# Gate/up, down and the last gate with output chunks in fours: products of 400 columns, and one part of the operand held while 512 weight columns pass

## The chip, the cores and the metric

The kernel runs on one core of one Trainium2 chip. The number that counts is the device time of one execution in microseconds (us), here as the median of several runs. Of the engines the text says PE for the matrix engine, ACT for the scalar engine, DVE for the vector engine; PEld is the loading of weights into the PE array, which the profile shows as a row of its own for each product. A "product" is one matmul instruction; its "columns" are those of its moving operand. "Native" products have fp32 operands; the others have operands in fp32r, a rounded 32-bit form of which the kernel writes a high part and a low part.

## What is computed

One decoder layer over 264 tokens: 256 of a prompt and 8 single-token sequences. Attention and a state-space group read one projection of the normed input; their results go through an output projection into the residual; then come a gated feed-forward block and a last gate. The stages that the change touches are the three last matrix stages:

```
h  = rms_norm(x, g_pre_ffn)
gu = h @ w_gate_up                                    # 2048 -> 2 x 5632
f  = (silu(gu[..., :D_FF]) * gu[..., D_FF:]) @ w_down # 5632 -> 2048
x  = x + rms_norm(f, g_post_ffn)
x  = x + sigmoid(x @ w_ple_gate) * (pe @ w_ple_proj)  # 2048 -> 2048
```

## The kernel before

Everything is kept transposed: a tile has 128 features on the partitions and the 264 tokens (`T`) as its columns. A matrix stage makes its output in chunks of 128 features, one PSUM bank for each (tile `acc`), and goes over the contraction in blocks of 128 (`k`). The stages of `stream_plan` are, in order: in, oa and os (the output projection), pp (first half), gu (gate/up: 88 chunks of 16 blocks), dn (down: 16 chunks of 44 blocks), pp (second half), pg (last gate: 16 chunks of 16 blocks). The 128x128 weight blocks are laid out in the order in which they are used, eight to a unit of 512 KB; there are 362 units of which the first six are used in native fp32.

Weights and operands are split, so that the products keep more than fp32r's precision: ACT writes the high part of a unit (`wh<-raw`, in `w_high`), DVE the rest (`wl<-raw,wh`, in `w_low`). The operand of a stage has a high tile and a low tile as well: `hh` and `hl` for gu, the two halves of `f0`/`f1` for dn, `x2h` and `x2l` for pg. For each weight block `stream` issues three products of 264 columns, all with the weight block as the stationary operand:

```
mm(ps, hi[:, b], xh, 0.1205, start=first, stop=False)
mm(ps, hi[:, b], xl, 0.1205, start=False, stop=False)
mm(ps, lo[:, b], xh, 0.1205, start=False, stop=last)
```

Most chunks are made one after the other (`chunks`); the first six of gu and of pg go side by side (`together`, with `EARLY`), block by block, while their operand is still being made. When a chunk is finished its epilogue runs: `epi_gu` multiplies a gate chunk and an up chunk out of PSUM by the norm factor (DVE tiles `gs` and `uu`, which frees both banks), applies SiLU on ACT, multiplies, and writes the two parts of `f`; `epi_dn` squares the chunk on ACT, copies it to `o2` and adds the square to `ssq_o` on DVE; `epi_pg` ends in the output.

The order of all instructions on all engines is set when the kernel is built: `Pace` keeps a clock for each engine and gives each piece of work that could go next a start time by costs that stand in the code (0.1205 for a product of 264 columns); the earliest goes first. PSUM banks are counted in `acc` and `bk`, 8 together. On the chip each engine keeps that order and waits on semaphores.

Between dn and pg stand the 16 pp products of the second half (eight chunks of two blocks, 48 products). In that stretch the chain that makes pg's operand must run: the last chunk's square, its sum over the partitions on PE (`ps_o<-sqd`), `rstd` on ACT and DVE (`n_y`, `n_t`, `Ro`), then for each block two DVE operations on `o2`, the high part `x2h` on ACT and the low part `x2l` on DVE.

## Time and profile before

| what | us |
|---|---|
| median of 3 runs | 1198.21 (1197.01 to 1201.53) |
| the profiled execution, its own time | 1203.08 |
| its span, first to last instruction | 1201.3 |
| PE busy / PEld busy | 1181.2 / 1154.4 |
| DVE busy / ACT busy | 754.0 / 587.1 |

The span is what the profile shows of one execution; the time of that execution is a little longer than its span. Products are pipelined on PE, so that rows overlap: a product's duration includes the way through the array, and what a product costs in a dense stretch is the distance from its start to the next one's start. Busy times of DVE and ACT can be read as they stand.

### The profile page before, as it was taken

To read this page: it belongs to the slowest core of one execution; us is meant where nothing else is said; L and a number is where in the kernel's file an instruction comes from. 1 tells how busy PE (TensorE), PEld (TensorE's weight loads), DVE (VectorE), ACT (ScalarE), POOL (GpSimd) and SP (SyncE) were. 2 spreads that over 40 slices of the span, in tenths; PEclk is the share of its full clock that TensorE was granted. 3 is DMA by queue.
4 is the path that set the end of the run, shared out by engine and by line. 5 is a ranking of instruction groups with operands and counts; after the bars stand their busy time and mean duration, and the time that the engine had idled before them with its cause. 6 is when DMAs were issued, how large, how long until landed. Compare 5 with 4: busy or idle time off the path is not lost.

```text
span 1201.3 us, 23874 instructions
## 1 busy us (share of the span) xinstructions
PE 1181.2 (98%) x9699; PEld 1154.4 (96%) x9699; DVE 754.0 (63%) x1325; ACT 587.1 (49%) x911; POOL 53.2 (4%) x97
## 2 busy tenths in 40 slices
PE   9899999999999999999999999999999999999998
PEld 7788888999999999999999999999999999999998
DVE  8998888867897555555555555555444444446864
ACT  6476857645665444444444444444434444435542
POOL 1122232000000000000000000000000000000000
PEclk9899999999999999999999999999999999999999
DMA  8745646666676666655555555555766666666683
GB/s 266 248 147 166 186 155 183 187 194 222 195 264 179 186 180 179 188 179 182 184 180 182 187 177 180 188 178 187 252 179 181 185 178 180 188 176 204 211 251 112
DMA packets 102214, 228.96 MB, mean 191 GB/s; under 512 B 26999, under 2 KB 50519, under 8 KB 101591
## 3 DMA queue, kind: packets, MB, share of 16 engines
q1 hardware_dynamic: 102103, 227.43, 61.6%
q8 instruction: 76, 1.25, 0.4%
q14 instruction: 35, 0.29, 0.1%
HBM read 214.60 MB, written 12.80 MB: 189 GB/s over the span
## 4 chain that ended last, share of the span: by engine, by line
PE 88%; DVE 7%; DMA 2%; ACT 1%; issue 1%; POOL 0%; SPq 0%; DVEq 0%; POOLq 0%; ACTq 0%
PE acc L285 82%; PE py L285 2%; DVE wl L222 1%; PE px L289 1%; DVE X L222 1%; DMA gt<-ys 1%; DVE rt L222 1%; DMA xtab<-in_xtab 0%; DMA xr<-in_x 0%; DVE ssq_x L222 0%; PE ph L975 0%; DVE sc L222 0%; DVE xl L222 0%; ACT s L281 0%; PE o L285 0%
## 5 line engine op out<-in xcount | busy, mean ns | idle before, releaser
L222 DVE TENSOR_TENSOR wl<-raw,wh 128x1024 fp32r<-128x1024 f32 x362 | 442.4, 1223 | 302.8 <-PE acc L285 281.3
L281 ACT ACTIVATE wh<-raw 128x1024 fp32r<-128x1024 f32 x362 | 383.8, 1060 | 449.2 <-PE acc L285 434.4
L285 PE MATMUL acc<-hh,wh 128*128 128x264 f32 x1408 | 399.5, 284 | 0.0
L285 PE MATMUL acc<-hl,wh 128*128 128x264 f32 x1408 | 398.3, 283 | 0.5 <-DVE hl L236 0.5
L285 PE MATMUL acc<-hh,wl 128*128 128x264 f32 x1408 | 398.5, 283 | 0.0
L285 PEld LDWEIGHTS acc<-hl,wh 128*128 128x128 f32 x1408 | 265.0, 188 | 0.8 <-DVE hl L236 0.7
L285 PEld LDWEIGHTS acc<-hh,wh 128*128 128x128 f32 x1408 | 265.2, 188 | 0.0
L285 PEld LDWEIGHTS acc<-hh,wl 128*128 128x128 f32 x1408 | 264.0, 188 | 0.0
L285 PE MATMUL acc<-f,wh 128*128 128x264 f32 x1408 | 256.8, 284 | 0.0
L285 PEld LDWEIGHTS acc<-f,wh 128*128 128x128 f32 x1408 | 217.8, 188 | 0.1
L285 PE MATMUL acc<-f,wl 128*128 128x264 f32 x704 | 199.7, 284 | 0.0
L285 PEld LDWEIGHTS acc<-f,wl 128*128 128x128 f32 x704 | 132.5, 188 | 0.0
L285 PE MATMUL acc<-x2h,wh 128*128 128x264 f32 x256 | 72.9, 285 | 0.0
L285 PE MATMUL acc<-x2h,wl 128*128 128x264 f32 x256 | 72.5, 284 | 0.0
L285 PE MATMUL acc<-xh,wh 128*128 128x264 f32 x240 | 72.5, 302 | 0.0
L285 PE MATMUL acc<-x2l,wh 128*128 128x264 f32 x256 | 71.9, 284 | 0.0
L285 PE MATMUL acc<-xl,wh 128*128 128x264 f32 x240 | 68.9, 287 | 2.3 <-DVE xl L222 2.3
L285 PE MATMUL acc<-xh,wl 128*128 128x264 f32 x240 | 68.7, 286 | 0.0
L222 DVE TENSOR_TENSOR uu<-acc,Rf 128x264 f32<-128x264 f32 x44 | 19.0, 432 | 50.6 <-PE acc L285 50.6
L285 PEld LDWEIGHTS acc<-xl,wh 128*128 128x128 f32 x240 | 46.0, 192 | 3.3 <-DVE xl L222 2.7
L285 PE MATMUL acc<-aops,wh 128*128 128x264 f32 x256 | 49.0, 291 | 0.0
L285 PEld LDWEIGHTS acc<-x2h,wh 128*128 128x128 f32 x256 | 48.1, 188 | 0.2 <-ACT ppt L281 0.2
(324 smaller groups left out, 1349.1 us busy)
## 6 DMA issues: line engine op xcount, KB each, us to landing
raw<-in_w SPq DMA_DIRECT2D x367, 512.0 KB, 3.6
T<-td SPq DMA_DIRECT2D x8, 512.0 KB, 4.6
xs<-in_x SPq DMA_DIRECT2D x2, 1056.0 KB, 7.1
ppd<-ppt SPq DMA_DIRECT2D x16, 132.0 KB, 3.2
x1d<-oo SPq DMA_DIRECT2D x4, 528.0 KB, 5.0
x<-x1d SPq DMA_DIRECT2D x2, 1056.0 KB, 7.3
ppr<-ppd SPq DMA_DIRECT2D x16, 132.0 KB, 4.0
xtab<-in_xtab SPq DMA_DIRECT2D x8, 256.0 KB, 3.0
```

Source lines behind the costliest of these rows:

```text
L222: V.tensor_tensor(out=out, in0=in0, in1=in1, op=op)
L281: S.activation(out=out, in_=in_, func=func, **kw)
L285: PE.matmul(out, lhsT, rhs, start=start, stop=stop)
L289: PE.transpose(out, in_, ident)
```

## The change

In gu, dn and pg the chunks go in groups of four, one weight block of each at a time. The operand of these stages now lies as one tile with the high part in columns 0 to 263 and the low part in columns 264 to 527 (`ha`/`hb`, `f0`/`f1`, `x2a`/`x2b`; `wide`). For four weight blocks of one contraction block there are now nine products in place of twelve:

- four of 400 columns ("a"): the high weights with the high part and the first 136 columns (`XE`) of the low part, written side by side into one bank;
- four of 264 columns ("b"): the low weights with the high part;
- one of 512 columns ("x"): the last 128 columns of the low part are the stationary operand, and the four high weight blocks pass as the moving operand. Its result stands the other way round (tokens on the partitions), in a bank of its own (`rows`).

At a group's end the rows bank is copied to SBUF by ACT (`held`), four products with a unit matrix ("c", 128 columns) add it, turned round, to the chunks' banks, and before the epilogue `whole` adds the 136 columns that stand apart: ACT copies them to `ext`, DVE adds them to the chunk. The last unit of a group is reordered (`last`) so that the rows are done early. Six chunks at the opening of gu and of pg go as one four and two in the old way (`six`); gu's chunks 3 and 47, and chunks 6 and 15 of pg, go in the old way; the last group of dn is a group of three beside one chunk in the old way. There are 28 groups.

In dn the last four chunks are copied to `o2` only after their squares. The write of `x1d` is a task of its own (`keep`).

The diff, cut to its core:

```diff
 def stream_plan():
...
+    def quad(at, gid, n=4):
+        r = []
+        for s in at:
+            r += [("a", s + i) for i in range(n)] + [("b", s + i) for i in range(n)] + [("x", s, gid)]
+            r += [("p", s + i) for i in range(n, 4)]
+        return r
+
+    def last(at, gid, between=(), n=4):
+        r = [("x", s, gid) for s in at] + list(between)
+        for i in range(n):
+            for s in at:
+                r += [("a", s + i), ("b", s + i)]
+            if i >= 2:
+                r += [("c", gid, j) for j in ((0, 1, 2) if i == 2 else (3,))]
+        return r + [("p", s + i) for i in range(n, 4) for s in at]
...
-    together("gu", EARLY["gu"], 16)
-    chunks("gu", [m for f in range(3, KF) for m in (f, KF + f) if m not in EARLY["gu"]], 16)
-    chunks("dn", range(16), KF)
+    six("gu", [0, KF, 1, KF + 1, 2, KF + 2], 16)
+    chunks("gu", [3, KF + 3], 16)
+    for f in range(4, KF, 2):
+        four("gu", [f, KF + f, f + 1, KF + f + 1], 16)
+    for m in range(0, 16, 4):
+        four("dn", list(range(m, m + 4)), KF, 4 if m < 12 else 3)
     chunks("pp", range(8, 16), 2)
-    together("pg", EARLY["pg"], 16)
-    chunks("pg", [m for m in range(16) if m not in EARLY["pg"]], 16)
+    six("pg", [0, 1, 2, 3, 4, 5], 16)
+    chunks("pg", [6], 16)
+    for m in (7, 11):
+        four("pg", list(range(m, m + 4)), 16)
+    chunks("pg", [15], 16)
...
+    def whole(ps):
+        yield "act", "+ext"
+        e = mid([P, XE], F32, "ext", "ext", 2)
+        act(e, ps[:, T:])
+        yield "dve"
+        add(ps[:, 0:XE], ps[:, 0:XE], e)
+        pace.rel("ext")
+
+    def held(gid):
+        yield "act"
+        rows[gid] = mid([P, 512], F32R, "rows", "rows", 2)
+        n = P * len(GROUPS[gid][1])
+        act(rows[gid][:, 0:n], rbank.pop(gid)[:, 0:n])
+        pace.rel("acc")
+        pace.sig(f"rows{gid}", "act")
...
+                        if what == "a":
+                            mm(ps, hi[:, b], x[:, 0:T + XE], 0.169, start=first, stop=False)
...
+                        elif what == "b":
+                            mm(ps[:, 0:T], lo[:, b], x[:, 0:T], 0.1205, start=False, stop=False)
+                        elif what == "x":
+                            n = P * len(GROUPS[more[0]][1])
+                            mm(ps[:, 0:n], x[:, T + XE:], hi[:, P * slot:P * slot + n], 0.422e-3 * n, start=first, stop=last)
...
+                        mm(ps[:, XE:T], rows[gid][:, P * j:P * j + P], ops["identr"], 0.1205, start=False)
```

How the instructions stand on the engines, before and after. First place: PE in the middle of gu, before. The rows are products, out<-moving,stationary, with the columns at the end; numbers tell buffers apart, and `acc_7630` and `acc_7691` are two chunks.

```order
L285 MATMUL acc_7630<-hh_4237,wh_7569 128x264
L285 MATMUL acc_7630<-hl_3642,wh_7569 128x264
L285 MATMUL acc_7630<-hh_4237,wl_7608 128x264
L285 MATMUL acc_7691<-hh_4237,wh_7603 128x264
L285 MATMUL acc_7691<-hl_3642,wh_7603 128x264
L285 MATMUL acc_7691<-hh_4237,wl_7636 128x264
```

The same place after the change: one contraction block of a group of four chunks. In the last row the weights are the moving operand.

```order
L358 MATMUL acc_5386<-hb_4239,wh_5465 128x400
L358 MATMUL acc_5390<-hb_4239,wh_5465 128x400
L358 MATMUL acc_5398<-hb_4239,wh_5465 128x400
L358 MATMUL acc_5400<-hb_4239,wh_5465 128x400
L358 MATMUL acc_5386<-hb_4239,wl_5489 128x264
L358 MATMUL acc_5390<-hb_4239,wl_5489 128x264
L358 MATMUL acc_5398<-hb_4239,wl_5489 128x264
L358 MATMUL acc_5400<-hb_4239,wl_5489 128x264
L358 MATMUL rows_5409<-wh_5465,hb_4239 128x512
```

Three products to a weight block, all of 264 columns, have become nine to four weight blocks. In all PE issues 1517 products fewer: the three stages had 7104 of 264 columns and now have 2720 of 264, 2188 of 400, 516 of 512 and 44 of 384, 8 of 136 (the "a" products of the two openings are cut in two) and 111 closing products of 128.

Second place: the end of a gu group after the change, on PE (the closing products of one group and the next group's first products).

```order
L358 MATMUL acc_5155<-identr_3643,rows_5362 128x128
L358 MATMUL acc_5159<-identr_3643,rows_5362 128x128
L358 MATMUL acc_5167<-identr_3643,rows_5362 128x128
L358 MATMUL acc_5169<-hb_4239,wh_5280 128x400
L358 MATMUL acc_5169<-hb_4239,wl_5306 128x264
```

After these rows the last two repeat for the second block, the fourth closing product follows, and then the next group's four products of 400, four of 264 and its first into a new rows bank. On DVE, at the same group's end (`ext` is the ACT copy of the 136 columns, and `uu` frees the two banks that it and `gs` read):

```order
L295 TENSOR_TENSOR wl_5354<-raw_5269,wh_5328 128x1024
L295 TENSOR_TENSOR acc_5155<-acc_5155,ext_5375 128x136
L295 TENSOR_TENSOR acc_5159<-acc_5159,ext_5378 128x136
L295 TENSOR_TENSOR gs_5392<-acc_5155,Rf_4241 128x264
L295 TENSOR_TENSOR uu_5393<-acc_5159,Rf_4241 128x264
L295 TENSOR_TENSOR acc_5167<-acc_5167,ext_5388 128x136
L295 TENSOR_TENSOR wl_5407<-raw_5293,wh_5352 128x1024
```

Two adds now stand ahead of `gs` and `uu`, where `gs` and `uu` stood alone; and a whole group ends at once, where chunks ended one by one.

Third place: PE between dn and pg, before, from dn's last product on (`ppo` is the operand of pp; x2 is two products alike).

```order
L285 MATMUL acc_12722<-f1_4864,wl_12811 128x264
L285 MATMUL acc_12896<-ppo_3741,wh_12809 128x264 x2
L285 MATMUL acc_12896<-ppo_3741,wl_12841 128x264
L285 MATMUL acc_12896<-ppo_3741,wh_12809 128x264 x2
L285 MATMUL acc_12896<-ppo_3741,wl_12841 128x264
L285 MATMUL acc_12908<-ppo_3741,wh_12809 128x264 x2
L285 MATMUL acc_12908<-ppo_3741,wl_12841 128x264
L285 MATMUL ps_o_12751<-sqd_12900,onesd_84 128x264
```

And after the change, around the same sum:

```order
L358 MATMUL acc_11914<-ppo_3743,wl_11828 128x264
L358 MATMUL ps_o_11924<-ssq_o_10140,onesd_84 128x264
L358 MATMUL ps_o_11924<-sqd_11904,onesd_84 128x264
L358 MATMUL acc_11914<-ppo_3743,wh_11800 128x264 x2
L358 MATMUL acc_11914<-ppo_3743,wl_11828 128x264
```

Of the 48 pp products 9 stood ahead of `ps_o<-sqd` and 39 behind it; now 27 stand ahead and 21 behind it.

## Rows read from the trace of the kernel before

**Rows 1.** The page: busy time of PE, and the chain that ended last.

```profile
PE 1181.2 (98%) x9699; PEld 1154.4 (96%) x9699; DVE 754.0 (63%) x1325; ACT 587.1 (49%) x911; POOL 53.2 (4%) x97
...
PE 88%; DVE 7%; DMA 2%; ACT 1%; issue 1%; POOL 0%; SPq 0%; DVEq 0%; POOLq 0%; ACTq 0%
PE acc L285 82%; PE py L285 2%; DVE wl L222 1%; PE px L289 1%; DVE X L222 1%; DMA gt<-ys 1%; DVE rt L222 1%; DMA xtab<-in_xtab 0%; DMA xr<-in_x 0%; DVE ssq_x L222 0%; PE ph L975 0%; DVE sc L222 0%; DVE xl L222 0%; ACT s L281 0%; PE o L285 0%
```

**Rows 2.** Windows: length, busy of PE, PEld, DVE, ACT, POOL; PEclk, DMA, GB/s.

```profile
600.00:700.00 100.00, 100.00 (x830) 100.00 (x829) 54.18 (x68) 42.25 (x51) 0.00 (x0) 1.00 0.56 183
900.00:1000.00 100.00, 100.00 (x826) 100.00 (x825) 43.91 (x40) 41.17 (x48) 0.00 (x0) 1.00 0.63 180
```

**Rows 3.** The page's groups: products of gu, dn and pg.

```profile
L285 PE MATMUL acc<-hh,wh 128*128 128x264 f32 x1408 | 399.5, 284 | 0.0
...
L285 PE MATMUL acc<-f,wh 128*128 128x264 f32 x1408 | 256.8, 284 | 0.0
...
L285 PE MATMUL acc<-f,wl 128*128 128x264 f32 x704 | 199.7, 284 | 0.0
...
L285 PE MATMUL acc<-x2h,wh 128*128 128x264 f32 x256 | 72.9, 285 | 0.0
```

**Rows 4.** By tile: duration of products in ns, min/median/max.

```profile
L285 PE MATMUL acc<-hh,wl x1408: 278/283/294, 327.4 to 839.6; 128*128 128x264 f32 x176
L285 PE MATMUL acc<-f,wl x704: 278/283/290, 840.0 to 1096.6; 128*128 128x264 f32 x176
```

**Rows 5.** By tile: the same of native products, two records each.

```profile
L285 PE MATMUL acc<-xt,raw x96: 386/386/490, 6.7 to 30.8; 128*128 128x264 f32 x96
```

**Rows 6.** Timeline of PE, native products: start, length, how many records.

```profile
27.47 3.72 PE L285 MATMUL acc<-xt,raw 128*128 128x264 f32 x16
```

**Rows 7.** Timeline of PE around 45 us.

```profile
45.10 0.42 PE L285 MATMUL acc<-xl,wh 128*128 128x264 f32 x1
...
46.86 0.42 PE L285 MATMUL acc<-xh,wh 128*128 128x264 f32 x1
```

**Rows 8.** Windows: the same stretch.

```profile
44.80:46.90 2.10, 2.10 (x12) 2.10 (x11) 2.10 (x9) 1.06 (x1) 0.00 (x0) 0.50 0.44 104
```

**Rows 9.** Timeline of PEld around a wait at gu's opening.

```profile
331.55 0.19 PEld L285 LDWEIGHTS acc<-hh,wh 128*128 128x128 f32 x1
332.48 0.19 PEld L285 LDWEIGHTS acc<-hl,wh 128*128 128x128 f32 x1 [0.74 <-DVE hl L236]
```

**Rows 10.** By tile: the product at 331.67, the last ahead of that wait.

```profile
L285 PE MATMUL acc<-hh,wh x1: 279/279/279, 331.7 to 331.7; 128*128 128x264 f32 x1
```

**Rows 11.** Timeline of PEld: weight loads of 128 columns for products of 128 columns.

```profile
97.39 1.86 PEld L285 LDWEIGHTS py<-G,SB 128*128 128x128 f32 x16 [0.17 <-issue]
```

**Rows 12.** Groups on ACT.

```profile
L281 ACT ACTIVATE wh<-raw 128x1024 fp32r<-128x1024 f32 x362 | 383.8, 1060 | 449.2 <-PE acc L285 434.4 <-DMA raw<-in_w 11.6 <-issue 2.5
...
L281 ACT ACTIVATE gy<-py 128x512 f32<-128x512 f32 x8 | 4.8, 599 | 8.4 <-PE py L285 8.3
...
L281 ACT ACTIVATE ht<-ph 128x128 f32<-128x128 f32 x8 | 2.2, 275 | 1.0 <-PE ph L975 1.0
```

**Rows 13.** Groups on DVE.

```profile
L222 DVE TENSOR_TENSOR wl<-raw,wh 128x1024 fp32r<-128x1024 f32 x362 | 442.4, 1223 | 302.8 <-PE acc L285 281.3 <-issue 14.3 <-ACT wh L281 2.8
L222 DVE TENSOR_TENSOR uu<-acc,Rf 128x264 f32<-128x264 f32 x44 | 19.0, 432 | 50.6 <-PE acc L285 50.6
...
L222 DVE TENSOR_TENSOR t<-p,xtab 128x128 f32<-128x128 f32 x8 | 2.3, 288 | 4.9 <-PE p L289 4.9
```

**Rows 14.** Timeline of PE between dn and pg.

```profile
1096.58 0.29 PE L285 MATMUL acc<-f,wl 128*128 128x264 f32 x1
...
1097.80 0.61 PE L285 MATMUL ps_o<-sqd,onesd 128*128 128x264 f32 x2
...
1102.96 0.28 PE L285 MATMUL acc<-x2h,wh 128*128 128x264 f32 x1
```

**Rows 15.** Timeline of ACT in the same stretch: the first high parts of pg's operand.

```profile
1101.88 0.77 ACT L281 ACTIVATE x2h<-o 128x264 fp32r<-128x264 f32 x2
```

More of the change, by code (lines that the diff above doesn't have):

```diff
@@ L393, in build @@
     ops = {}
+    wide = {}
     XF = {}
@@ L1516, in need_op, with finish, end @@
             return f"x2_{k}"
+        def finish(nm, m, ps):
+            ready = pace.t["pe"] + 0.2
+            def end():
+                if (nm, m) in FOURS:
+                    yield from whole(ps)
+                yield from EPI[nm](ps[:, 0:T], m)
+            pace.add(end(), ready=ready, prio=PRIO["epi"])
         def stream():
@@ L1544, in stream @@
                     yield "pe", need
+                    if not native:
+                        lo = lows.get(ui)
                     if key not in jobs:
-                        jobs[key] = bank([P, T], "acc")
-                        if nm == "pg" and m + 1 >= len(EARLY["pg"]):
-                            for i in range(len(EARLY["pg"])) if m + 1 == len(EARLY["pg"]) else [m]:
+                        jobs[key] = bank([P, 512 if what == "x" else T + XE if key in FOURS else T], "acc" if what != "x" else "rows")
+                        if nm == "pg" and what != "x":
+                            for i in (4, 5, 0, 1, 2, 3) if m == 0 else [m] if m > 5 else []:
@@ L1549, in stream @@
                                 pace.add(fetch_pp(i), prio=4)
                     ps = jobs[key]
-                    first, last = kc == 0, kc == NK[nm] - 1
-                    if late and kc:
-                        yield "pe", late[0][0]
-                        for _, f in late:
-                            f()
-                        late.clear()
-                    b = slice(128 * k, 128 * k + 128)
                     if native:
                         mm(ps, raws[ui][:, b], XF["t"][:, kc, :], 0.446, start=first, stop=last)
-                    else:
+                    elif nm not in wide:
@@ L1572, in stream @@
+                    if last and what == "p":
+                        finish(nm, m, ps)
                 if native:
```

187 lines of the change are left out of this document (126 added, 61 removed).

## The prediction

> **What bounds the kernel now.** I read the page first. PE is busy 98% of the span, and the chain that ended last runs 88% over PE, 82% of it over the products into `acc` [rows 1]. The windows come next: in the middle of gu and of dn PE and PEld never stop, the granted clock is 1.00, DVE is busy 54% and 44% and ACT 42% and 41%, DMA about 0.6 [rows 2]. So in the three stages nothing but the distance from one product to the next counts, and work put on DVE or ACT is free as long as PE does not wait for it. 830 and 826 products start in 100 us, which is 120.5 and 121.1 ns each; I use 120.7. The page's groups give the counts: 3 x 1408 products in gu, 1408 + 704 in dn, 3 x 256 in pg, 7104 in all [rows 3], or 857 us of the span.
>
> The step that decides the forecast is to split these 120.7 ns. At half clock (granted 0.50, so 1.2 GHz) [rows 8] the same products follow each other at exactly 220 ns: 1.76 us for eight steps [rows 7], and 264 columns at 1.2 GHz are 220.0 ns. So a column takes one cycle. At full clock (2.4 GHz) 264 columns take 110.0 ns, and 10.7 ns of each product are not columns. All that the change can win lies in these 10.7 ns, because the columns stay: 2188 x 400 + 516 x 512 + 44 x 384 + 8 x 136 + 2720 x 264 is 1,875,456, and 7104 x 264 is the same number.
>
> **The change part by part.**
>
> *Fewer products.* Without the closing ones there are 5476 in place of 7104, so 1628 fewer. What that is worth depends on how the extra goes with length, and no product of this kind with another length stands in the trace. Three readings are possible. If every product pays 10.7 ns whatever its length, the gain is 1628 x 10.7 = 17.4 us. If the extra belongs to short products only, the wide ones pay what a native record pays: two passes of 264 columns are 220.0 ns, and 16 records in 3.72 us less the last one's 0.386 [rows 5, 6] are 222.3 ns apart, so 2.3 ns. Then the extra falls from 7104 x 10.7 = 76.0 us to 2720 x 10.7 + 2748 x 2.3 + 0.4 (the eight short ones) = 35.8 us, a gain of 40.2. If the extra goes with the columns (0.457 ns a column in place of 0.417), the gain is nothing.
>
> I take the first, by two rows. A native record lasts 386 ns, 166 more than its columns [rows 5]; that is the way through the array. Taken off the 278 to 294 ns (median 283) of the fp32r products [rows 4] it leaves 112 at the least, 117 in the middle and 128 at the most for the same 264 columns. A rate below one column a cycle would not allow 112, so the extra is hardly by column. And the product at 331.67, after which no weights were loaded until 332.48 [rows 9], lasts 279 [rows 10], so 113: part of the extra is there with no load running beside the product, so a wide product will not lose all of it by giving the next load more time. The nearest row to a product of 400 fp32r columns is one of 264 fp32r columns, with the same operands and loads.
>
> The Trainium skill ("TensorE: Matmul & The Clock Gate", section "Wait — 56ns, not 53.3ns?") gives each warm product about 2.5 ns beyond its columns, at any length. The trace disagrees for fp32r, 10.7 against 2.5, and agrees for the native records, 2.3. By the page the 1628 products would be worth 4.1 us, and with its 55.8 ns for each of the 111 closing products, 6.2 us, the change would cost about 2 us before its waits.
>
> *The closing products.* 111 of 128 columns. Their bound from below is 53.3 + 10.7 = 64 ns; but each needs weights of 128 columns loaded first, and such loads start 111 ns apart even for products of 107 ns (two passes of 128 columns): 16 in 1.86 us, less 0.19 for the last, over 15 [rows 11]. From above 121, as before. I take 112: +12.4 us (7.1 to 13.4). This eats most of the gain.
>
> *ACT and DVE.* 111 copies `ext` by the 275 ns of 128x128 and 28 copies of rows by the 599 of 128x512 [rows 12] are 47 us on ACT; 111 adds by 288 [rows 13] are 32 us on DVE. Over some 750 us both engines have over 40% free [rows 2], so it costs nothing unless PE waits at a group's end. There are two such places, at 24 ends where a group follows a group.
>
> The first is the closing product, which needs the rows copied. The copy can start some 0.4 us after the last "x" started (213 ns of columns, 166 through the array) and takes 0.6, so about 1.05 with its semaphores. The rest of that "x" and twelve products of three chunks lie between, 0.22 + 6 x (0.177 + 0.121) = 2.0 us. If ACT has just begun a `wh` of 1.06 us [rows 12] there is about nothing left. I take no wait.
>
> The second is the next group's first "x", which is the ninth bank and needs one back from `uu`. From the first closing product that is 0.28 us until it has landed, 0.3 for `ext`, 0.3 for the add, the second pair shifted by 0.2, and two operations out of PSUM of 0.43, which overlap a little [rows 13], with three semaphores about 2.0 us. PE has 0.34 + 4 products + 0.11 + 4 x 0.177 + 4 x 0.121 = 2.2 us until then. Hidden, by 0.2 us only; a wait here is a rival below.
>
> *Between dn and pg.* Before, dn's last product starts at 1096.58, `ps_o<-sqd` at 1097.80 and pg's first product at 1102.96 [rows 14]; the first `x2h` begins at 1101.88 and is there after half of its two, at about 1102.3 [rows 15]. So the chain from `ps_o<-sqd` needs 4.5 us and had 5.2. Now four chunks end together, their four squares and the added columns come first, and `ps_o<-sqd` stands behind 27 products of pp; what is left as cover is that native product, 0.45, and 21 products of pp, 2.5 us. PE waits about 1.5 us. Bounds: 0, if ACT and DVE are freer than before and the chain shrinks to 3 us, and 3, if the squares come later than `ps_o`'s place.
>
> *The rest.* The same 362 units pass, `x1d` goes out on SP's queue as before, and nothing waits for it but `f0`; the opening of gu has the same products block by block. Nothing.
>
> **Sum**, against the profiled execution's own 1203.08: -17.4 + 12.4 + 1.5 = -3.5, so 1199.6. That execution is 4.9 above the median of the runs, so in terms of the median 1194.7. I say 1195, or 0.3% less: no change that can be told (0.5%, 6 us, is about what a measurement of this kernel can tell).
>
> **Rivals.**
>
> *Wide products lose the extra.* The extra is then the price of a weight load that does not quite fit beside 110 ns of columns. For it speaks that PEld is busy without a break [rows 2], that loads of 128 columns cannot be closer than 111 [rows 11], and that native products, with 220 ns for each load, pay 2.3 [rows 6]; against it the product with no load behind it [rows 10]. -40.2 + 12.4 + 1.5 = -26.3: 1172. Half of the extra gone would give 1183. The Trainium skill (same page, section "Back-to-back issue gap") says that the spacing of load and product pairs is set by both, which is the rule for this case; that no row shows a wide fp32r product leaves it open.
>
> *The extra goes by columns.* Slower than before: nothing won, 12.4 to 13.4 us of closing products and 1.5 of waiting, so 1212. For it: only fp32r at full clock, which reads a new 4-byte column each cycle, has the extra, native records and half clock do not [rows 5 to 8]. Against it: the 112 ns. It decides from about 0.43 ns a column on, where less than 10 us are left of the gain.
>
> *The banks come back late.* If DVE has begun a `wl` of 1.22 us [rows 13] just as the first `ext` arrives, "x" waits up to 1 us; half of that at 24 ends is 12 us, so 1207. From 0.15 us an end on, the change wins nothing. For it: the 0.2 us of cover and a `wl` right ahead of the adds in DVE's order; against: DVE is idle almost half of the time there [rows 2].
>
> **Chances.** Forecast (every product pays) 0.44, between 1188 and 1203 by the bounds of closing products, waits and 1 ns more or less of extra; wide products lose all or half of it 0.30, 1166 to 1186; by columns 0.14, 1206 to 1216; banks 0.12, 1203 to 1215. Below 1192.2 (faster) lie the second and a third of the first: 0.44. Above 1204.2 (slower) lie the third, most of the fourth and little of the first: 0.26. Within 0.30. From 1170 to 1214 about a tenth is left out below and less above.
>
> **What would show it.** In the profile after: (1) in the middle of gu the number of products in 100 us. One contraction block of four chunks takes 4 x 177.4 + 4 x 120.7 + 224 = 1417 ns by the forecast (635 products in 100 us), 1375 by the first rival (655), 1448 by the second (622). (2) The starts of "a", "b" and "x" apart: 177, 121, 224 against 169, 121, 216 or 183, 121, 234. (3) Closing products 112 apart. (4) Waits of PE for `rows` or for `uu`: none of over 0.3 us an end. (5) One wait of 1 to 2 us ahead of pg's first product. What would make it wrong most of all is (2): no row before shows an fp32r product of another length.

## The result, and the profile after

The changed kernel takes 1211.53 us (median of 4, 1211.33 to 1213.73) beside 1198.5 (1197.01 to 1201.53) of the kernel before on the same chip: a ratio of 1.011, 95% interval 1.0087 to 1.0133. It is slower by 13.0 us (1.1%) where 3.5 less were forecast. The profiled execution took 1211.49 us.

The page of the changed kernel, to be read beside [rows 1]: busy time, and the chain that ended last.

```profile
PE 1189.2 (98%) x8182; PEld 1139.2 (94%) x8182; DVE 771.4 (64%) x1436; ACT 622.6 (51%) x1051; POOL 51.6 (4%) x97
...
PE 87%; DVE 8%; DMA 1%; issue 1%; ACT 1%; POOL 0%; SPq 0%; DVEq 0%; ACTq 0%; POOLq 0%
```

The bound is the one that it was, PE from product to product. There are 1517 products fewer, and PE is busy 8 us longer.

Windows in the middle of gu and of dn, beside [rows 2]:

```profile
600.00:700.00 100.00, 100.00 (x627) 96.95 (x626) 55.14 (x83) 46.78 (x71) 0.00 (x0) 1.00 0.54 178
900.00:1000.00 100.00, 100.00 (x624) 96.90 (x623) 46.84 (x51) 43.23 (x61) 0.00 (x0) 1.00 0.55 181
```

PE never stops, the clock is full, PEld has now some idle time, DVE and ACT have a little more to do. 627 products in 100 us is near the 622 of the second rival; the forecast was 635, the first rival 655. (These counts, those of [rows 2] too, take in the two or three products that are still running when the window begins.) By the starts in the trace, a group of four gu chunks was 192 products 120.8 ns apart, 23.20 us; now it is 148 with its closings, 23.65 us. In dn it was 528, 64.2 us, and is 400, 64.3 us. So the steps of nine and the closings together cost as much as the twelve did, and a little more.

Timeline of PE, one contraction block of a gu group and the start of the next (start, length, what, how many records):

```profile
600.71 0.89 PE L358 MATMUL acc<-hb,wh 128*128 128x400 f32 x4
601.44 0.65 PE L358 MATMUL acc<-hb,wl 128*128 128x264 f32 x4
601.93 0.39 PE L358 MATMUL rows<-wh,hb 128*128 128x512 f32 x1
602.16 0.91 PE L358 MATMUL acc<-hb,wh 128*128 128x400 f32 x4
```

Worked out from the starts of all such steps, the mean distance to the next product is in gu 184.3 ns for "a", 121.7 for "b" and 231.3 for "x", 1455.5 for the nine, where twelve of before take 1450. In dn it is 183.2, 121.5 and 233.6, 1452 for the nine, where twelve take 1459. The forecast had 177, 121, 224; the rival by columns had 183, 121, 234.

The profiled execution of before entered gu some 7 us later than the same kernel ahead of the second probe below (327.3 against 320.7 us); its granted clock was 0.66 there from 40 to 50 us and 0.97 from 50 to 100, where the other has 0.83 and 1.00. For a balance by stage I therefore take that other execution. Windows by stage, that execution first: gu's opening, the rest of gu, dn, up to pg, pg to the end.

```profile
320.60:356.60 36.00, 35.45 (x291) 35.25 (x291) 35.81 (x63) 24.31 (x46) 0.00 (x0) 1.00 0.76 253
356.60:833.10 476.50, 476.50 (x3942) 476.37 (x3941) 265.08 (x340) 207.45 (x252) 0.00 (x0) 1.00 0.58 182
833.10:1090.20 257.10, 257.10 (x2118) 257.03 (x2117) 114.63 (x106) 104.86 (x122) 0.00 (x0) 1.00 0.58 189
1090.20:1096.30 6.10, 6.10 (x51) 6.03 (x50) 4.85 (x11) 5.62 (x14) 0.00 (x0) 1.00 0.71 242
1096.30:1194.70 98.40, 94.01 (x770) 93.58 (x768) 65.30 (x108) 42.83 (x63) 0.00 (x0) 1.00 0.64 197
```

The same stages of the changed kernel:

```profile
320.80:359.50 38.70, 37.08 (x250) 34.99 (x249) 36.59 (x66) 25.50 (x48) 0.00 (x0) 1.00 0.75 244
359.50:844.90 485.40, 485.40 (x3064) 471.26 (x3062) 273.94 (x416) 232.36 (x352) 0.00 (x0) 1.00 0.54 179
844.90:1102.20 257.30, 257.30 (x1646) 251.37 (x1645) 118.79 (x125) 108.13 (x139) 0.00 (x0) 1.00 0.57 188
1102.20:1110.60 8.40, 7.07 (x54) 6.55 (x52) 6.91 (x15) 7.83 (x21) 0.00 (x0) 1.00 0.71 208
1110.60:1209.70 99.10, 94.91 (x640) 92.57 (x640) 67.19 (x120) 46.13 (x78) 0.00 (x0) 0.99 0.58 189
```

Of the lengths the opening is up by 2.7, the rest of gu by 8.9, dn by 0.2, the stretch up to pg by 2.3, pg by 0.7. Together that is 14.8; the medians differ by 13.0. Most of the loss is in a stretch where PE has no gap at all. PE's waits in the changed kernel that bear on the three stages (us in total, times, longest):

```profile
PE acc L358 <- ACT x2a L354: 1.3, 1, 1.3
...
PE acc L358 <- DVE hb L309: 1.1, 2, 0.8
...
PE rows L358 <- DVE hb L309: 0.5, 1, 0.5
```

None is at a group's end. The one at gu's opening before:

```profile
PE acc L285 <- DVE hl L236: 0.5, 1, 0.5
```

### The profile page after: what moved, and what is told of

It is laid out like the page before. It is cut to its first block, busy times and chain, and to the rows that moved or that the text cites. A ratio compares the mean times of both kernels' runs of the same rounds, so it can differ in the third digit from the quotient of the medians.

```text
span 1209.7 us, 21196 instructions
## 1 busy us (share of the span) xinstructions
PE 1189.2 (98%) x8182; PEld 1139.2 (94%) x8182; DVE 771.4 (64%) x1436; ACT 622.6 (51%) x1051; POOL 51.6 (4%) x97
## 4 chain that ended last, share of the span: by engine, by line
PE 87%; DVE 8%; DMA 1%; issue 1%; ACT 1%; POOL 0%; SPq 0%; DVEq 0%; ACTq 0%; POOLq 0%
PE acc L358 71%; PE rows L358 10%; PE py L358 2%; DVE wl L295 2%; PE px L362 1%; DVE X L295 1%; PE s L358 1%; DVE rt L295 1%; DMA xtab<-in_xtab 0%; PE pt L362 0%; DVE ssq_x L295 0%; PE o L358 0%; PE ph L1050 0%; PE pw L358 0%; DVE xl L295 0%
## 5 line engine op out<-in xcount | busy, mean ns | idle before, releaser
L358 PE MATMUL acc<-hb,wh 128*128 128x400 f32 (+1 forms) x736 | 179.0, 342 | 1.1 <-DVE hb L309 1.1
L358 PE MATMUL acc<-f,wh 128*128 128x400 f32 (+1 forms) x748 | 168.6, 338 | 0.0
L358 PE MATMUL acc<-ha,wh 128*128 128x400 f32 (+1 forms) x740 | 163.6, 341 | 0.0
L358 PEld LDWEIGHTS acc<-hb,wh 128*128 128x128 f32 x736 | 134.6, 188 | 8.2 <-issue 1.2
L358 PEld LDWEIGHTS acc<-ha,wh 128*128 128x128 f32 x740 | 132.8, 188 | 6.4 <-DVE ha L309 0.3
L358 PEld LDWEIGHTS acc<-f,wh 128*128 128x128 f32 x748 | 133.3, 188 | 5.6
L358 PE MATMUL acc<-hb,wl 128*128 128x264 f32 x704 | 137.9, 284 | 0.0
L358 PE MATMUL acc<-ha,wl 128*128 128x264 f32 x704 | 118.2, 285 | 0.0
L358 PEld LDWEIGHTS acc<-hb,wl 128*128 128x128 f32 x704 | 114.9, 188 | 1.2
L358 PEld LDWEIGHTS acc<-ha,wl 128*128 128x128 f32 x704 | 109.4, 188 | 0.3
L295 DVE TENSOR_TENSOR acc<-acc,ext 128x136 f32<-128x136 f32 x111 | 30.4, 302 | 42.0 <-ACT ext L354 42.0
```

The costliest lines, as they stand in the source:

```text
L295: V.tensor_tensor(out=out, in0=in0, in1=in1, op=op)
L358: PE.matmul(out, lhsT, rhs, start=start, stop=stop)
```

## The experiments

All but the probes are compared with the kernel before on the same chip. The probes are rows of products alone, appended behind the last output of the kernel before, with DVE, ACT and DMA idle.

### Products of other lengths alone

32 products in a row of 264, 400, 512 and 128 columns over the operand of pg, and controls.

```diff
+            go("t264", 264, wt, mv)
+            go("t400", 400, wt, mv)
+            go("t512", 512, wt, mv)
+            go("t128", 128, wt, mv)
+            go("s512", 512, lambda i: w[:, 128 * i:128 * i + 32], mv, m=32)
+            go("z512", 512, lambda i: z[:, 128 * i:128 * i + 128], lambda i, n: z[:, 0:n])
...
+            go("f512", 512, lambda i: w[:, 0:128], lambda i, n: xf[:, 0:n])
```

> The kernel before, with ten rows of products added behind its last one, each row into a bank of its own, PE alone at work (no ACT, DVE or weight traffic): fp32r products of 264, 400, 512 and 128 columns with 128 weight columns (t264, t400, t512, t128), of 512 with 32 weight columns (s512), of 512 with weights and operand all zero (z512), bf16 of 264 and 512 (h264, h512), 512 with one weight block and one address throughout (f512), native fp32 of 264 (n264). Start to start, in ns. Theory 'rate': an fp32r column costs more than a cycle at full clock, at any length, from the form itself: t264 121, t400 182, t512 231, s512, z512 and f512 231 as well, h264 113 and h512 216. Rival 'other engines': the extra comes from what ACT, DVE and DMA read and write meanwhile; alone t264 is 113, t400 169, t512 216. Rival 'weight loads': loads and columns get in each other's way; s512, with a quarter of the load, is well below t512 (about 220). Rival 'data': with nothing but zeros z512 is 216 while t512 is 231. Rival 'address': f512 differs from t512 by more than 5. The theory of the forecast (10.7 ns for every product at any length) would have t400 177 and t512 224.

Worked out from the starts in the trace, mean distance at full clock:

```
264: 121.3 ns   400: 181.6   512: 232.4   128: 111.7
512, weights of 32 columns: 232.2   512, zeros: 227.9   512, one place, one weight block: 227.4
bf16 264: 112.5   bf16 512: 215.9   native 264, a record: 222.4
```

The loss shows with nothing else running, so neither DVE, ACT nor the bank is its cause. The size of the weight load is not either (232.2 with a quarter of it). The bf16 products take their columns and 2.5 ns, so it is the fp32r form. 121.3, 181.6 and 232.4 lie on a line of 0.448 ns a column, and I took that for the rival by columns. The 227.4 and 227.9, 5 ns less at one place, did not fit it.

### The closing products left out

```diff
-                        mm(ps[:, XE:T], rows[gid][:, P * j:P * j + P], ops["identr"], 0.1205, start=False)
...
-                            mm(ps[:, 0:T], lo[:, b], x[:, 0:T], 0.1205, start=False, stop=False)
+                            mm(ps[:, 0:T], lo[:, b], x[:, 0:T], 0.1205, start=False, stop=last)
```

> The changed kernel without the 111 closing products; it leaves out the part that they add (low part of the last 128 tokens in the chunks in fours), all else stays, the copies of the rows too. In the changed kernel's trace these products are followed by the next one after 86 ns in the mean. Theory 'rate': nine products cost as much as twelve, so the closings are most of the loss: 9 to 10 us less than with them, 1202, still 3 above the kernel before. Rival 'waits at the group ends': the copies and adds hold PE up there, and the products themselves are cheap: under 4 us less, 1208 or more. By the forecast's 112 ns each: 12.4 less, 1199.

1225.34 us (1224.33 to 1227.47), ratio 1.0226 (1.0209 to 1.0243): slower than with them. Waits of PE behind the opening:

```profile
PE rows L358 <- DVE gs L295: 10.8, 20, 0.5
PE acc L358 <- ACT x2a L354: 3.7, 1, 3.7
```

Without closings the next group's "x" is due earlier, and at 20 ends PE waits about 0.5 us for its bank, which the epilogue on DVE still reads. But the run changed more than the closings: the order of instructions is set when the kernel is built, and on DVE it came out otherwise. Timeline of DVE at the end of the same group, in the changed kernel (its next "x" starts at 444.05):

```profile
442.78 0.42 DVE L295 TENSOR_TENSOR gs<-acc,Rf 128x264 f32<-128x264 f32 x1
443.12 0.42 DVE L295 TENSOR_TENSOR uu<-acc,Rf 128x264 f32<-128x264 f32 x1
443.46 0.30 DVE L295 TENSOR_TENSOR acc<-acc,ext 128x136 f32<-128x136 f32 x1
443.67 1.22 DVE L295 TENSOR_TENSOR wl<-raw,wh 128x1024 fp32r<-128x1024 f32 x1
```

and without closings, then PE's "x" there:

```profile
443.11 1.23 DVE L295 TENSOR_TENSOR wl<-raw,wh 128x1024 fp32r<-128x1024 f32 x1 [0.60 <-PE acc L358]
444.26 0.42 DVE L295 TENSOR_TENSOR gs<-acc,Rf 128x264 f32<-128x264 f32 x1
444.60 0.42 DVE L295 TENSOR_TENSOR uu<-acc,Rf 128x264 f32<-128x264 f32 x1
```

```profile
444.83 0.47 PE L358 MATMUL rows<-wh,ha 128*128 128x512 f32 x1 [0.54 <-DVE gs L295]
```

A `wl` now stands ahead of `gs` and `uu`: the bank rival, with the cause that the prediction gave it. In the changed kernel `uu` ends 0.50 us ahead of "x" at each of these ends, more than the 0.34 us that the four closings take; whether the bank would come late without them in the old order was not tried. By the starts gu is 5.8 us longer than in the changed kernel, the stretch up to pg 4.1. So the run could not price the closings.

### The closing products done twice

```diff
+                        mm(ps[:, XE:T], rows[gid][:, P * j:P * j + P], ops["identr"], 0.1205, start=False, stop=False)
                         mm(ps[:, XE:T], rows[gid][:, P * j:P * j + P], ops["identr"], 0.1205, start=False)
```

> The changed kernel with each of its 111 closings done twice (the held part is added twice, so that part of the result is doubled). In the changed kernel a closing begins on average 86 ns ahead of the next product, between 60 and 112. If closings lie on TensorE's own path: 111 x 86 to 112 ns = 9.5 to 12.4 us more, 1221 to 1224. If they fill a wait (leaving them out opened waits for the bank in place of a gain): under 4 us more, 1212 to 1215.

1227.45 us (1227.08 to 1229.35), ratio 1.0239 (1.0224 to 1.0255), 15.9 us more than the changed kernel, so the closings lie on PE's path. Windows, middle of gu:

```profile
600.00:700.00 100.00, 100.00 (x631) 96.96 (x630) 54.77 (x82) 46.75 (x70) 0.00 (x0) 1.00 0.53 174
```

A group is 152 products now and by the starts takes 24.14 us in place of 23.65, so 0.12 us for each added closing; times 111 that is 13.5. By stages of the two profiled executions, 0.8 us are lost ahead of gu, 9.9 in gu with 84 added closings, 1.7 in dn with 15, 0.8 up to pg (PE waits 2.4 there in place of 1.3) and 2.7 in pg with 12, about 1.3 more than these 12 explain; that remainder I did not place.

### Fours in down alone

```diff
-        four("gu", [f, KF + f, f + 1, KF + f + 1], 16)
+        chunks("gu", [f, KF + f, f + 1, KF + f + 1], 16)
...
-        four("pg", list(range(m, m + 4)), 16)
+        chunks("pg", list(range(m, m + 4)), 16)
```

The openings of six and the wide operand tiles stay.

> The changed kernel with fours in down and in the two openings alone; the other 80 chunks of gate/up and 8 of the last gate go in the old way. 88 of the 111 closing products and 352 of the 560 nine-product steps fall away. Theory 'rate' (a step of nine costs 6 ns more than one of twelve, a closing 86 ns): 352 x 6 ns + 88 x 86 ns = 9.7 us less than the changed kernel, 1202. Rival 'one place' (the loss sits in the openings and between down and the last gate): no more than 2 us less, 1210.

1208.71 us (1207.4 to 1209.51), ratio 1.0083 (1.0068 to 1.0098). Both expectations missed what it showed. Windows, middle of gu, where the products are those of before again:

```profile
600.00:700.00 100.00, 100.00 (x820) 100.00 (x819) 53.47 (x67) 41.98 (x50) 0.00 (x0) 1.00 0.58 180
```

820 in place of 830. Same products, same order, same engines: only the operand's rows lie elsewhere, 528 columns (2112 bytes) apart in place of 264. That takes 1.4 ns a product, some 5.5 us for the 3936 products of gu behind its opening (an estimate), and so is a good part of what the changed kernel loses there. Against twelve products laid this way (1467 ns) its step of nine gains 11 ns. From here on the place of the rows was a suspect.

### Places and lengths

```diff
+            for name, s in zip(("va", "vb", "vc", "vd", "ve", "vf", "vg", "vh"), range(0, 64, 8)):
+                go(name, 264, [s])
...
+            for name, s in zip(("wa", "wb", "wc", "wd"), (0, 8, 16, 32)):
+                go(name, 400, [s])
+            for name, s in zip(("xa", "xb", "xc", "xd"), (0, 8, 16, 32)):
+                go(name, 512, [s])
+            for name, n in zip(("ya", "yb", "yc", "yd"), (256, 272, 288, 320)):
+                go(name, n, [0])
```

> The kernel of before, with rows of products alone behind its end: 264, 400 and 512 columns that start s columns into the moving tile, s from 0 to 64, 20 of one start in a row, then rows that go between two starts and walk by 264, 272 and 320 columns. Theory 'addresses': the gate/up product of before and of the kernel with only the down groups have one time per place in the program, to 0.3 ns, between 116 and 129 ns, with a period of 8 chunks where chunks lie 1056 bytes apart and of 4 where they lie 2112 apart, so the place of the moving rows modulo 256 bytes sets it; then rows of one start differ by several ns with s, s 0 and s 64 agree to 0.5 ns, and some start is at 116 ns or less. Theory 'steps': what matters is the jump from one product's rows to the next; then rows of one start all take the same and only the rows that alternate or walk differ. Theory 'columns alone': all rows of 264 columns take 121 +- 1 ns, of 400 columns 182 +- 1, of 512 columns 232 +- 1.

Timeline of PE, rows of 20 products:

```profile
1231.40 3.77 PE L285 MATMUL wa<-x2h,pw_w 128*128 128x400 f32 x20
1235.01 3.76 PE L285 MATMUL wb<-x2h,pw_w 128*128 128x400 f32 x20
...
1245.88 4.72 PE L285 MATMUL xa<-x2h,pw_w 128*128 128x512 f32 x20
1250.43 4.83 PE L285 MATMUL xb<-x2h,pw_w 128*128 128x512 f32 x20
1255.10 4.75 PE L285 MATMUL xc<-x2h,pw_w 128*128 128x512 f32 x20
...
1264.34 2.56 PE L285 MATMUL ya<-x2h,pw_w 128*128 128x256 f32 x20
1266.73 2.67 PE L285 MATMUL yb<-x2h,pw_w 128*128 128x272 f32 x20
...
1271.88 3.10 PE L285 MATMUL yd<-x2h,pw_w 128*128 128x320 f32 x20
1274.81 2.56 PE L285 MATMUL za<-x2h,pw_w 128*128 128x264 f32 x20
```

From one row's start to the next one's, over 20: 512 columns begun at 0 take 227.5 ns, begun 8 columns (32 bytes) later 233.5. Without the first few products of a row, which still settle, the starts in the trace give 119.7 to 120.0 at 256 columns, 146.7 at 320, 180.0 to 180.4 at 400 and 226.7 at 512: 13.3 ns beyond the columns each time, and 120.0, 10.0 beyond, at 264. At other starts 264 takes up to 123.5, 400 up to 183.1, 512 up to 233.3. 272 and 288 columns, tried at start 0 alone, took 125.6 and 131.7, 12.3 and 11.7 beyond. So the surplus is not by column: at the best place it is 13.3 ns at 256, 320, 400 and 512 columns alike, at others up to 20, and 264 is a cheap length. Averaged over the starts that were tried it is 11.4 ns at 264, 14.2 at 400 and 16.9 at 512, so a wide product does pay more on the average, though less than in proportion. 'Columns alone' falls. Of 'addresses' one part did too: no place gave 116 or less on the mean, and starts 0 and 64 (256 bytes apart) differed by 1.6.

### The kernels' own orders, alone

```diff
+            row("na", nine(528, 8), 2)
+            row("nb", nine(576, 7), 2)
+            row("nc", nine(576, 7, 32), 2)
+            row("nd", three(264, 8 * 264, 8), 4)
+            row("ne", three(320, 6 * 320, 6), 5)
+            row("nf", three(528, 264, 8), 4)
```

> Rows of products alone behind the kernel of before, in the orders that the kernels use: the step of nine (4 x 400, 4 x 264, 1 x 512 columns) with operand rows every 528 columns as the changed kernel has them (na), every 576 (2304 bytes, nine times 256; nb), and that begun 32 columns later (nc); triples of 264 with rows every 264 (nd, as in before), every 320 (1280 bytes; ne) and every 528 (nf); triples with the two correction products in bf16 (ng, nh); 512 (ni), 400 (nj, nk) and 264 (nl, nm) alone with rows every 528 and 576. Theory 'places': a row begun at a place that a product likes costs columns / 2.4 GHz plus 10 ns at 264 and 13.3 ns at 256, 320, 400 and 512, one begun elsewhere up to 20 ns; then nb takes 1427 to 1437 ns a step against about 1452 for na, ne 120 ns a product against 120.7 for nd and about 122 for nf, nk 180 against 182 to 183 for nj. Theory 'columns': na, nb and nc agree within 4 ns a step, nd, ne and nf within 0.3 ns. Triples with bf16: (120 + 2 x 112.5) / 3 = 115 ns a product if the two forms do not disturb each other.

Timeline of PE, the first rows of each:

```profile
1205.98 1.38 PE L285 MATMUL na<-x2h,pw_w 128*128 128x400 f32 x8
...
1229.23 1.37 PE L285 MATMUL nb<-x2h,pw_w 128*128 128x400 f32 x8
...
1249.31 1.38 PE L285 MATMUL nc<-x2h,pw_w 128*128 128x400 f32 x8
...
1269.96 5.23 PE L285 MATMUL nd<-x2h,pw_w 128*128 128x264 f32 x42
...
1281.56 5.62 PE L285 MATMUL ne<-x2h,pw_w 128*128 128x264 f32 x45
```

A step of nine takes 23.25 us / 16 = 1453 ns as the changed kernel has it, 20.08 / 14 = 1434 with rows 576 columns apart, 20.65 / 14 = 1475 with those begun 128 bytes later (1480 once settled, of which "x" takes 254, where it takes 231 to 233 in the other two). The sign and size are those of 'places'; but triples with rows 320 apart (ne, 121.3) are no better than those of before (nd, 120.8), which it had not said. Triples with rows 528 apart took 121.7 (122 expected). Alone, 400 columns took 182.1 with rows 528 apart and 180.2 with 576, as expected, but 264 took 121.5 with either. The bf16 triples took 120.6 a product once settled, not 115: a change of form costs what the form saves, if it comes at every product.

### Rows of 576 columns in the changed kernel

```diff
-                X2["h"] = [big.tile([P, 8, 2 * T], F32R, tag="X3", name="ha")]
+                X2["h"] = [big.tile([P, 8, XW], F32R, tag="X3", name="ha")]
...
-            X2["h"].append(big.tile([P, 8, 2 * T], F32R, tag="X1", name="hb"))
+            X2["h"].append(big.tile([P, 8, XW], F32R, tag="X1", name="hb"))
```

> The changed kernel with the gate/up operands (and the second half of those of the last gate) in rows of 576 columns in place of 528, so that each begins at the same place modulo 256 bytes; one buffer of squares less at the start pays for the space. Theory 'places': a step of nine in gate/up falls from 1454 ns to 1430 to 1440, times 336 steps 5 to 8 us less: 1204 to 1207 us against 1211.5, with 633 to 637 products in 100 us of gate/up where there were 627. Theory 'columns': 1210 to 1213, 627 products.

1206.55 us (1206.24 to 1208.66), ratio 1.0061 (1.0043 to 1.0079), 5.0 less than the changed kernel. Windows, gu and dn:

```profile
600.00:700.00 100.00, 100.00 (x632) 97.31 (x631) 55.55 (x82) 47.67 (x71) 0.00 (x0) 1.00 0.55 179
900.00:1000.00 100.00, 100.00 (x624) 96.90 (x623) 46.52 (x50) 43.15 (x61) 0.00 (x0) 1.00 0.55 180
```

632 for 627 in gu, where the rows were moved, just under the 633 to 637 expected, and 624 as it was in dn, where they were not. By the starts gu is 4.3 us shorter and dn as long as it was; a step of nine in gu takes 1443.5 ns on average in place of 1455.5. "x" now lies 225 ns ahead of its successor (231), "b" 120.5 (121.7), and "a" 184.0, nearly as before (184.3). Where the rows lie is shown to be a cause, in the kernel itself.

### Everything moved, and the weights alone

224 unused bytes ahead of all tiles, or between operands and weights:

```diff
+    shift = const.tile([P, 56], F32, name="shift")
     gains = const.tile([P, 80], F32, name="gains")
```

```diff
+    gap_p = ctx.enter_context(tc.tile_pool(name="gap", bufs=1))
+    gap = gap_p.tile([P, 56], F32, name="gap")
     raw_p = ctx.enter_context(tc.tile_pool(name="raw", bufs=NRAW))
```

> The kernel of before with 224 unused bytes ahead of its tiles, so that weights and operands begin at 0 modulo 256 bytes where they began at 32; rows keep their 264 columns. Theory 'places' gives a size, not a sign: the time of each place in the eight-chunk pattern of gate/up changes by some ns, the mean of 120.8 ns by up to +-1 ns, and with 7104 such products the kernel by up to +-7 us. Theory 'columns': 1198.5 +- 1.5, the same pattern.

> The kernel of before with 224 unused bytes between the operands and the weights' buffers: operands begin at 32 modulo 256 bytes as before, weights at 0 where they began at 32 too (moving both left the time as it was; in the last probe moving the operands alone by this distance took a triple's products from 120.2 to 122.2 ns, moving both gave 120.4). Theory 'relative': gate/up shows fewer than 830 products in 100 us, down to 818, and with 4224 + 768 such products (down's later operands move with the weights) the kernel takes up to 9 us more: 1200 to 1208. Theory 'jumps' (only the distance of one product's moving rows from the next counts): 830 products, 1198.5 +- 1.5.

1199.73 us (ratio 1.0001, 0.9986 to 1.0015) and 1197.14 (0.9987, 0.9976 to 0.9998), 830 products in 100 us of gu in both. The times tell nothing, the pattern does. Mean distance in ns from each of a contraction block's three products to the next one, over the last 60 gu chunks, worked out from the starts in the traces (blocks 0 to 7; 8 to 15 repeat them):

```
block        0                  1                  2                  3
before       120.7 115.9 120.0  121.0 123.1 119.3  123.6 121.4 120.7  118.6 120.0 118.3
all moved    120.9 116.0 120.0  121.0 123.0 119.1  123.6 121.4 120.9  118.4 120.0 118.6
weights only 121.0 123.1 119.3  123.6 121.4 120.7  118.6 120.0 118.3  118.1 120.0 120.0
block        4                  5                  6                  7
before       118.1 120.0 120.0  124.3 121.6 122.0  118.0 120.0 122.7  129.3 120.0 121.4
all moved    118.0 120.0 120.0  124.1 121.9 121.7  118.3 120.0 122.4  129.3 120.0 121.4
weights only 124.3 121.6 122.0  118.0 120.0 122.7  129.3 120.0 121.4  120.7 115.9 120.0
```

Moved together, operands and weights keep the pattern; with the weights moved against the operands it turns by one block, and one block is 32 bytes modulo 256. So a product's time depends on how its moving rows lie against the weights, modulo 256 bytes, as 'relative' has it. 'Jumps' had no turn, and 'places', which went by the operand's own bytes, would have turned with the first shift. My price for the second, up to 9 us, was wrong: rows 264 columns apart go through all eight places whatever the offset, so the mean stays. That the period is 256 bytes rests on this turn and on the eight blocks; in the rows of one start alone, above, two places 256 bytes apart still differed by 1.6 ns. Rows 528 apart visit four, rows 576 apart one, and then the choice shows.

### The same alone, and units of one form at a time

```diff
+            row("qa", three(0, 0), 5)
+            row("qb", three(8, 8), 5)
+            row("qc", three(0, 8), 5)
+            row("qd", three(8, 0), 5)
+            row("qe", three(32, 0), 5)
+            row("ra", unit(8), 4)
```

> Rows of products alone behind the kernel of before. Five rows of triples of 264 with operand rows every 264 columns: weights and operands as they lie (qa), both begun 8 columns (32 bytes) later (qb), only the operands later (qc), only the weights later (qd), weights 32 columns later (qe). Moving the whole kernel by 32 bytes changed no place of its pattern (830 products in 100 us both ways). Theory 'relative': a product's time depends on how its moving rows lie against the weights that are loaded meanwhile; qa and qb then show the same pattern to 0.3 ns a place, qc, qd and qe other ones. Theory 'jumps': only the distance from one product's moving rows to the next ones counts; all five are alike. Theory 'clock places': qa and qb differ as qa and qc do. Then units of 8 chunks, eight fp32r products and after them sixteen in bf16 (ra), in fours (rb) and twos (rc), eight and sixteen all in fp32r (rd), bf16 alone (re): a change of form costs about 361.7 - 120 - 225 = 17 ns for both ways by the triples of the last probe, so ra takes 2783 ns for 24 products (116.0 each), rb 116.7, rc 118, rd 120.8, re 112.5; if a bf16 product beside fp32r weights is slower for other reasons, ra stays at 120.

By the starts in the trace: qa 120.2 ns a product, qb 120.4, qc 122.2, qd 120.9, qe 121.2, which is for 'relative' again (not to 0.3 ns at each place: these rows of seven blocks did not settle into one pattern). Eight fp32r products and then sixteen in bf16 take 115.4 to 116.3 a product, in fours 116.8, in twos 118.2, bf16 alone 112.5; eight and sixteen all in fp32r 121.9.

### A faster version: the corrections in bf16

The kernel before, without fours. In gu, dn and pg a unit's eight products of high weights and high operand come first, then its sixteen correction products in bf16.

```diff
+                yield "act", [f"raw{i}", "+wl"]
+                lows[i] = wl_p.tile([P, 2048], BF16, tag="wl", name="wb")
+                act(lows[i][:, 0:1024], raws[i])
...
+                            if step == 0:
+                                mm(ps, highs[ui][:, b], xh, 0.1205, start=first, stop=False)
+                                continue
+                            lo = lows[ui]
+                            mm(ps, lo[:, b], xx[:, T:], 0.1125, start=False, stop=False)
+                            mm(ps, lo[:, 1024 + 128 * k:1152 + 128 * k], xx[:, 0:T], 0.1125, start=False, stop=last)
```

> The kernel of before (no groups of four) with the two correction products of gate/up, down and last gate in bf16: a bf16 copy of the weights made by ScalarE, the low weights and the low operand rounded to bf16, a bf16 copy of the high operand; eight fp32r products of a unit first and then its sixteen bf16 ones. The results differ in the last bits that the corrections carry. Theory 'the surplus belongs to the fp32r form' (264 columns: 120.7 ns, bf16 112.5): 16 x 8.2 less 17 for the change of form is 115 ns a unit, times 296 units 34 us: 1165 us, range 1160 to 1175, with 862 products in 100 us of gate/up. If ScalarE at 1.22 + 0.94 us a unit of 2.8 does not keep ahead of TensorE: 1175 to 1200, with waits of PE on ACT.

> The same with the bf16 copy of the weights made by GpSimd, which is idle in these stages. As with ScalarE if the copy of 1024 columns stays under 2.7 us and does not hold up VectorE: 1165 us; else 1175 to 1230 with waits of PE on POOL or DVE.

1171.18 us with the copy on ACT (1170.11 to 1174.75), ratio 0.9765 (0.974 to 0.979): faster than both kernels. With the copy on POOL 1186.42 (1185.7 to 1186.8), 0.9894 (0.9874 to 0.9915). Windows in gu with ACT's copy, and PE's wait for the low weights:

```profile
600.00:700.00 100.00, 100.00 (x866) 90.43 (x865) 57.24 (x72) 80.62 (x99) 0.00 (x0) 1.00 0.62 190
```

```profile
PE acc L287 <- DVE wb L224: 1.2, 3, 0.5
```

866 products in 100 us, 115.7 ns apart; 862 were expected. The gain is 28 us where 34 were: at gu's opening PE waits 4.8 us in all, and the granted clock there is 0.83 to 0.94 in three of six windows of 10 us. With POOL's copy the middle of gu goes at the same 866, but at the openings of gu and of pg PE waits for the low weights. Its waits, and the page's groups of the copy and of DVE's low part:

```profile
PE acc L287 <- DVE wb L224: 12.7, 10, 2.0
```

```profile
L266 POOL CAST wb<-raw 128x1024 bf16<-128x1024 f32 x296 | 385.7, 1303 | 559.8 <-PE acc L287 480.1
...
L224 DVE TENSOR_TENSOR wb<-raw,wh 128x1024 bf16<-128x1024 f32 x296 | 476.7, 1642 | 30.1 <-PE acc L287 14.8
```

The same subtraction on the page of the kernel with the copy on ACT:

```profile
L224 DVE TENSOR_TENSOR wb<-raw,wh 128x1024 bf16<-128x1024 f32 x296 | 361.1, 1223 | 241.0 <-PE acc L287 221.6
```

It takes 1642 ns on average with POOL at work beside it, 1223 without.

## Why the prediction was wrong

**What bounds the kernel** held: in gu and dn the distance between products alone counts, and the copies and adds, 43.9 us on ACT and 30.4 on DVE (47 and 32 forecast), cost PE nothing at the groups' ends. The 120.5 and 121.1 ns a product were a little low, since the window's count holds products begun before it; by the starts it is 120.8 and 121.6.

**The step that failed** is "every product pays 10.7 ns whatever its length". I took it because the shortest record, less the 166 ns of a native one, left 112 ns and a rate by column would not allow that. But a record's length tells no rate. Less 166 it falls 3 to 4 ns short of the distance to the next product at every length (117.4 against 120.8 in gu before, 180.5 against 184.7 for 400 columns and 227.4 against 231.2 for 512 after), and it varies as the distances do, which in gu lie anywhere from 116 to 129 at one and the same length by where the rows lie; at one place alone they go 117, 123, 117, 123 around a mean of 120.0. What the runs put in its place: alone and at good places, 264 columns are the cheap length (10.0 ns) and 256, 320, 400 and 512 pay 13.3; and where the changed kernel lays its rows in gu, "a" pays 17.7, "b" 11.7 and "x" 17.9. So a step's nine pay 4 x 17.7 + 4 x 11.7 + 17.9 = 135 ns, where the twelve of before paid 130, and of the 17.4 us nothing is left. (In dn the nine pay 132 and the twelve paid 139.) In numbers of the kernel: the rest of gu is 8.9 us longer, of which the 80 closings take 6.9 at 86 ns (9.7 by the price of an added one), so 320 steps cost -0.8 to +2.0 us, not the -10.3 forecast; 320 times the 5.5 ns between the two steps is 1.8. A good part of it is the wide tile: the old triples on its rows pay 12.2 ns each, 147 for twelve.

**The closing products** were priced at 112. From a closing's start to the next product's are 86 ns on average, 9.6 us for 111; an added one costs 0.12 us, by which the 111 would be 13.5. The forecast's 12.4 lies between. That they lie on PE's path is shown. They are also part of the cover under which the bank comes back, but the cover does not hang on them: 0.50 us were left of it.

**The waits at a group's end**: none, as forecast, and with 0.50 us of cover where 0.2 was estimated (the rows' copy is done 0.56 us before the first closing). The run without closings shows that the bank rival was real once a `wl` stands ahead of `gs` and `uu`.

**Between dn and pg** 1.5 us of waiting were forecast; PE waits 1.3, and the stretch is 2.3 longer.

**"The rest: nothing"** was wrong at gu's opening, 2.7 us: PE now waits 1.6 us for `hb`, which DVE writes, where it waited 0.5 for `hl`; the other 1.6 us of the 2.7 I did not place. That the order of six meets the second half of the operand sooner is argued only; it wasn't tried apart.

**The rivals.** 1212 and 622 products were the numbers of "the extra goes by columns", which got 0.14, and the kernel came out at 1211.5 and 627. Its mechanism is not the one: 256, 320, 400 and 512 columns pay the same at the best place. Its number came out by luck: places and lengths together happen to leave nothing, as it had it for another reason. "Wide products lose the extra" is refuted: 400 and 512 columns pay 13 ns and more, and with weight loads of 32 columns 512 still take 232.2. The forecast's 12.4 and 1.5 us for closings and waits were near what was measured, so the miss is in the main the 17.4 us.

At the best places a step would take 4 x 180.0 + 4 x 120.0 + 226.7 = 1427 ns, an estimate from the second probe, against twelve at 120.8, 1450: 11.8 us for the 516 steps of four chunks, no more than the closings and the new waits cost. The kernel with 576 columns a row, whose step in gu takes 1443.5, still loses 0.6% to before.

## What to carry to other kernels

Before products are merged into wider ones, time rows of the new lengths alone, on the chip, with the operand laid as it will lie; a scatter of single records says nothing of a cost by length. In a stage that only PE bounds, the pitch of operand rows against the weights is a parameter like any other: 1434 to 1475 ns for the same nine products. And here the corrections, which need few bits, were better in bf16, kept together by form, than in cleverly fewer fp32r products: 28 us won against 13 lost. A run that leaves something out can also change the order in which the rest is built, so look at that order before a price is read from it.

## What the runs showed of the hardware that was not expected

- fp32r products at full clock settle, at good places, at 120.0, 146.7, 180.0 and 226.7 ns for 256 or 264, 320, 400 and 512 columns. All four are whole multiples of 6.67 ns, the time of 16 columns; why wasn't tried.
- How an fp32r product's moving rows lie against the weights sets its time. In gu of before the distance to the next product goes from 115.9 to 129.3 ns with a period of eight blocks, and its mean at each place is the same to 0.3 ns when everything is moved together; rows of one start settle at 120.0 to 123.5 ns for 264 columns, 180.0 to 183.1 for 400 and 226.7 to 233.3 for 512.
- bf16 takes 112.5 ns for 264 columns and 215.9 for 512, 2.5 and 2.6 beyond the columns. The Trainium skill ("TensorE: Matmul & The Clock Gate", section "Wait — 56ns, not 53.3ns?") gives about 2.5 at any length: the runs agree for bf16 and not for fp32r, 10 to 20.
- A change between fp32r and bf16 products and back costs about 17 ns (triples of one and two: 361.7 ns where 345 would be the sum).
- POOL casts of 1303 ns beside it make DVE's subtraction of 1024 columns a third longer (1642 ns against 1223).
